# Long branch A of a two-branch encoder layer: three of eight units transposed by VectorE and DRAM, with TensorE's order held

## The chip, the cores and the metric

The kernel runs on one core of one Trainium2 chip. The metric is the device time of one execution in microseconds (us), median of the runs. TensorE (PE) multiplies matrices, VectorE (DVE) and ScalarE (ACT) work elementwise, GpSimd (POOL) helps them, SyncE (SP) issues most DMAs. Lines such as L829 are lines of the kernel before.

## The reference

One encoder layer runs on two sequences with the same weights: `x_prompt` (1024 tokens) and `x_sample` (512 tokens), width 1024, all in float32.

```python
z = rmsnorm(x) @ W_in   # q_A k_A v_A q_B k_B v_B gate_A gate_B
o_A = grouped-query attention: 8 query heads in 2 groups of 4, one key/value head a group,
      head width 64, softmax over all keys, no mask
o_B = neighbourhood attention on the 64-wide token grid, with a position bias
mix = (sigmoid(gate_A) * (o_A @ W_pA) + sigmoid(gate_B) * (o_B @ W_pB)) @ W_out
x = x + mix;  x = x + relu(rmsnorm(x) @ W_up)**2 @ W_down;  y = rmsnorm(x)
```

What the change touches is `o_A` of the 1024-token sequence: for each group, softmax(q k^T / 8) v with 4 heads x 1024 queries x 1024 keys.

## The kernel before

Every float32 operand is used as a sum of two fp32r parts, a rounded one ("hi") and the rest ("lo"), and a product is made of two or three matmuls (`mm3`: hi*hi, hi*lo, lo*hi; the helper `mul`, L212, issues each). The function `run` does the attention part of one sequence, the 512-token one first (`NB` = 1), then the 1024-token one (`NB` = 2, `N` = "s1"). After both comes the MLP for all tokens.

For each of the two groups `g`, a phase "R" projects and rotates q, k and v, and a phase "A" does the attention (L773 to L804 and on). In phase A of the long sequence:

- A **unit** is one head with 512 queries: 4 heads x 2 query blocks = 8 units a group. `NT` = 8 key chunks of 128.
- `s_tile(u, j)` makes the scores of 128 queries against 1024 keys: four 512-column matmuls into a two-bank PSUM tile `s` (two such tiles exist), a VectorE maximum (L788), a ScalarE Exp with row sums (L791), a VectorE reciprocal (L793) and a GpSimd multiplication in place (L794). The result `p` has queries on partitions; eight buffers of it exist.
- For PV the keys must be on partitions. For each key chunk `kc`, TensorE transposes four 128x128 blocks into one PSUM bank (L829), ScalarE copies it as the rounded part (L834), and VectorE subtracts for the rest (L835).
- `pv(u, kc, hi, lo)` adds two 512-column matmuls into the unit's accumulator bank (L805, L806), two chunks behind the transposes (`LAG`). After the eighth, `finish_o` adds the two halves on ScalarE and VectorE (L474, L483) and writes 128 KB to DRAM.
- `fill.pull(n)` takes n steps of other TensorE work: here the gate projection (`gate`), three 512-column matmuls a step.
- In unit u, the four score tiles of unit u+1 are made in chunks 0, 1, 3 and 4.

PSUM has eight banks: four for the two score tiles and four (`mm`) for transposes, accumulators and the gate's sums. A pool of eleven 8 KiB-per-partition buffers (`slot`) holds two activation tiles, q, k and v (four), the gate's weights and whatever comes next.

The order of instructions on each engine is set by a scheduler that works at build time: among instructions that are ready by its own reckoning it takes the one that comes first in the program. `tc.keep_in_program_order` chains an instruction to the earlier ones so marked on the same engine; `tc.issue_after(x)` puts an instruction behind x on x's engine. While `held_pe` is not empty, `mul` chains all TensorE work. Before the change only branch B of the long sequence sets it (the neighbourhood attention, phase "B"), and there most units are already transposed in another way: VectorE transposes 32x32 blocks in place (L1100), the tile is written to DRAM (`tbs`, L1103), read back with its blocks regrouped (`bhs`, L1110), rounded by ScalarE (L1122) and subtracted by VectorE (L1123). For these units the Exp (L1088) writes its result in runs of 32 elements, in an order that makes the regrouping read long runs. The last eight units of branch B are transposed by TensorE, and there the Exp writes every fourth element.

In phase A of the long sequence nothing is held. `put` issues the writes of gates and outputs on ScalarE's DMA queue, unless `slot_no` is set; then they go to a list `later_put`, which SyncE issues later.

## Time and profile before

| | us |
|---|---|
| median of 3 runs | 2127.22 (2126.32 to 2127.64) |
| the profiled execution | 2126.34 |
| its span, first to last instruction | 2124.5 |
| phase A of the long sequence, group 0 | 451.0 to 582.4 in the span |
| phase R of group 1 | 582.4 to 643.5 |
| phase A of the long sequence, group 1 | 643.5 to 774.0 |
| branch B of the long sequence, from its first score matmul | 797.8 on |

The granted TensorE clock is 0.999 of full speed over the span. In the profile's rows, "xcount | busy, mean ns | idle before" gives the time in which at least one instruction of a group ran, the mean duration of one, and how long the engine sat idle just before them with what ended that. Durations of matmuls overlap: a matmul starts before the one in front of it has drained, so the time TensorE needs for one is read from start to start. In a timeline row, the first number is the start in the span, the second the duration, and a row with x4 merges four in a run.

### The profile page before, as it was taken

The numbers are of one execution on the slowest core, as the hardware profiler recorded it, in microseconds if no ns is written. First come the engines' busy times: TensorE is split into PE (matmuls) and PEld (weight loads), VectorE is DVE, ScalarE is ACT, GpSimd is POOL, SyncE is SP. The second block draws the span as 40 slices with busy tenths as digits, with TensorE's granted clock in tenths as the row PEclk, the third lists the DMA queues.
The fourth block names the chain that finished last, engine by engine and source line by source line (L and its number), as shares of the span: only waits on it lengthen the run. The fifth ranks groups of instructions, "written<-read, shape, count | busy, mean of one in ns | idle before, by whom it ended". The sixth has DMA issues, their size and how long they took to land.

```text
span 2124.5 us, 31728 instructions
## 1 busy us (share of the span) xinstructions
PE 2096.5 (99%) x10871; PEld 1839.0 (87%) x10871; DVE 1480.0 (70%) x2793; ACT 1145.7 (54%) x2487; POOL 363.3 (17%) x446
## 2 busy tenths in 40 slices
PE   9999999999999999999999999999999999999998
PEld 8888778888898888887888999999999988888887
DVE  6666786777647756777873877778777777669563
ACT  6665653666666745556531566666565643334452
POOL 2232310332232314443101100002000000000000
PEclk9999999999999999999999999999999999999999
DMA  6436557530122136876563656568454899688561
GB/s 191 133 99 200 160 150 256 192 86 23 49 70 87 45 84 193 241 224 193 172 227 124 199 181 206 163 230 214 156 162 146 272 350 341 213 280 278 164 204 64
DMA packets 336104, 372.92 MB, mean 176 GB/s; under 512 B 31039, under 2 KB 267207, under 8 KB 335943
## 3 DMA queue, kind: packets, MB, share of 16 engines
q1 hardware_dynamic: 297463, 305.60, 45.6%
q10 hardware_dynamic: 31328, 45.11, 6.2%
q0 software_dynamic: 7152, 20.19, 3.5%
q8 instruction: 86, 1.41, 0.3%
q14 instruction: 75, 0.61, 0.1%
HBM read 274.29 MB, written 97.32 MB: 175 GB/s over the span
## 4 chain that ended last, share of the span: by engine, by line
PE 52%; DVE 1%; issue 0%; ACT 0%; POOLq 0%; POOL 0%; ACTq 0%; DVEq 0%
PE dn L212 20%; PE ua L212 6%; PE ud L212 6%; PE uc L212 6%; PE ops L212 4%; PE ub L212 3%; PE ppbs L212 2%; PE ppas L212 2%; PE dnf L212 2%; PE pt L353 1%; PE obs L212 0%; PE ptbs L1132 0%; ACT pbs L1088 0%; PE sbs L212 0%; DVE A L1458 0%
## 5 line engine op out<-in xcount | busy, mean ns | idle before, releaser
L212 PE MATMUL dn<-wd,ah 128*128 128x512 f32 x1248 | 384.2, 389 | 0.0
L212 PEld LDWEIGHTS dn<-wd,ah 128*128 128x128 f32 x1248 | 234.2, 188 | 48.7
L212 PE MATMUL dn<-wd,al 128*128 128x512 f32 x624 | 242.8, 389 | 0.0
L1457 ACT ACTIVATE ah<-ar 128x512 fp32r<-128x512 f32 x168 | 104.4, 627 | 206.7 <-PE dn L212 185.6
L212 PE MATMUL gpss<-xs_0h,w_gs 128*128 128x512 f32 x512 | 189.4, 402 | 0.8 <-DVE ot_Bs L471 0.4
L1458 DVE TENSOR_TENSOR al<-ar,ah 128x512 fp32r<-128x512 f32 x168 | 114.1, 687 | 76.4 <-ACT ah L1457 66.6
L212 PE MATMUL ud<-B,A 128*128 128x384 f32 x768 | 143.7, 334 | 0.7 <-DVE c L1575 0.7
L212 PE MATMUL uc<-B,A 128*128 128x384 f32 x768 | 143.7, 334 | 0.0
L212 PE MATMUL ua<-B,A 128*128 128x384 f32 x768 | 138.8, 334 | 0.0
L212 PEld LDWEIGHTS dn<-wd,al 128*128 128x128 f32 x624 | 117.1, 188 | 24.2
L794 POOL TENSOR_SCALAR ps<-ps,rls 128x1024 f32<-128x1024 f32 (+1 forms) x96 | 96.8, 1009 | 228.4 <-DVE rls L793 213.8
L212 PEld LDWEIGHTS ud<-B,A 128*128 128x128 f32 x768 | 134.0, 188 | 1.1 <-DVE c L1575 1.1
L212 PEld LDWEIGHTS uc<-B,A 128*128 128x128 f32 x768 | 134.1, 188 | 0.2 <-ACT A L1457 0.2
L834 ACT ACTIVATE pths<-pTs 128x512 fp32r<-128x512 f32 x160 | 94.1, 597 | 73.9 <-PE pTs L829 71.3
L212 PEld LDWEIGHTS ua<-B,A 128*128 128x128 f32 x768 | 133.7, 188 | 0.2
L835 DVE TENSOR_TENSOR ptls<-pTs,pths 128x512 fp32r<-128x512 f32 x160 | 107.5, 686 | 37.7 <-ACT pths L834 36.7
L212 PE MATMUL ops<-wh_os,mgs 128*128 128x512 f32 x384 | 119.4, 390 | 0.0
L788 DVE TENSOR_REDUCE nms<-ss 128x1 f32<-128x1024 f32 (+1 forms) x96 | 99.8, 1040 | 25.0 <-PE ss L786 24.5
L212 PEld LDWEIGHTS gpss<-xs_0h,w_gs 128*128 128x128 f32 x512 | 96.1, 188 | 19.0 <-DVE w_gs L206 0.7
L791 ACT ACTIVATE ps<-ss,nms 128x1024 f32<-128x1024 f32 (+1 forms) x96 | 93.3, 972 | 32.1 <-DVE nms L788 26.2
L180 POOL TENSOR_TENSOR rs_f<-ms_f,mhalf 128x1 f32<-128x1 f32 x6 | 4.0, 667 | 590.7 <-DVE ms_f L176 590.7
L829 PEld LDWEIGHTS pTs<-ident,ps 128*128 128x128 f32 x640 | 78.0, 140 | 28.4 <-POOL ps L794 4.4
(287 smaller groups left out, 5144.2 us busy)
## 6 DMA issues: line engine op xcount, KB each, us to landing
ar<-ud SPq DMA_DIRECT2D x120, 512.0 KB, 5.4
br<-in_w_mlp_down_dram SPq DMA_DIRECT2D x72, 512.0 KB, 5.3
rawu<-in_w_mlp_up_dram SPq DMA_DIRECT2D x64, 512.0 KB, 4.1
ud<-c ACTq DMA_DIRECT2D x128, 192.0 KB, 3.6
raw_gs<-in_w_in_dram SPq DMA_DIRECT2D x32, 512.0 KB, 3.9
ud<-cs SPq DMA_DIRECT2D x64, 192.0 KB
tbs<-pbs SPq DMA_DIRECT2D x24, 384.0 KB, 4.8
bhs<-tbs SPq DMA_DIRECT2D x24, 384.0 KB, 3.7
```

What stands on the lines that cost most here:

```text
L180: nc.gpsimd.tensor_tensor(r[:, :n], m[:, :n], mhalf[:, :n], op=ALU.pow)
L212: op = nc.tensor.matmul(out, a, b, **kw)
L353: nc.tensor.transpose(halves[c // 4][:, (c % 4) * P : (c % 4 + 1) * P], t[:, c * P : (c + 1) * P], ident)
L788: nc.vector.tensor_reduce(nm_, s, axis=AX.X, op=ALU.max, negate=True)
L791: op = nc.scalar.activation(p, s, AF.Exp, bias=nm_, accum_out=l)
L794: nc.gpsimd.tensor_scalar(p, p, rl, 1.0, op0=ALU.mult, op1=ALU.mult)
L829: nc.tensor.transpose(pt[:, j * P : (j + 1) * P], PP[u, j][:, kc * P : (kc + 1) * P], ident)
L834: nc.scalar.activation(hi, pt, AF.Copy)
L835: nc.vector.tensor_tensor(lo, pt, hi.bitcast(F32), op=ALU.subtract)
L1457: nc.scalar.activation(hi, src, AF.Copy)
L1458: nc.vector.tensor_tensor(lo, src, hi.bitcast(F32), op=ALU.subtract)
```

## The change

Units 1, 3 and 5 of each group of the long sequence are "turned". For them:

- the Exp reads every fourth column of the PSUM tile in its inner order and writes runs of 32 (`of`, `to`);
- `turn` transposes the tile's 32x32 blocks in place on VectorE (128 x 1024) and writes it to DRAM (512 KB); it is placed inside the next score tile, between the maximum and the Exp (`between`);
- `fetch` reads it back regrouped, two slots later, into a buffer for two tiles; both DMAs are on SyncE's queue, chained;
- `rounded` makes the rounded part on ScalarE, behind the latest Exp, and the rest by a subtract in place: tiles 0 and 2 on GpSimd, 1 and 3 on VectorE;
- `pv_pair` multiplies two tiles (256 queries) at a time: 8 chunks x 2 parts, 16 matmuls of 256 columns, with a stride in the moving operand.

Only the five other units are transposed by TensorE. `step` is one such unit, with its transposes in eight slots, one a key chunk. In the steps of units 0, 2 and 4 the slots carry the score tiles of the turned unit (0 to 3) and of the next plain one (4 to 7), and two gate pulls in the first four slots and one in the others. The first pair of a turned unit is multiplied at the end of the step, the second in slot 1 of the next one. In the step of unit 6 the tiles of unit 7 come in slots 0, 1, 3 and 4.

In both groups TensorE's order is held from the first score tile to the end, and gates and outputs are written by SyncE from `later_put`. The short sequence keeps the old loop. The diff, without the lines that only rename:

```diff
@@ -184,7 +184,7 @@
...
     def note(engine, op):
-        if held_pe:
+        if "B" in held_pe:
             firm[engine].append(op.ins)
@@ -772,9 +772,10 @@
...
                 units = [(h, qb) for h in range(4) for qb in range(NB)]
-                PP = {}
-
-                def s_tile(u, j):
+                PP, tA, fA, hA, last_exp = {}, {}, {}, {}, [None]
+                turned = {units[i] for i in (1, 3, 5)} if NB == 2 else set()
+
+                def s_tile(u, j, between=None):
                     h, qb = u
@@ -782,13 +783,20 @@
...
                         ks = slice(kb * 512, kb * 512 + 512)
-                        nc.tensor.matmul(s[:, ks], lhs, kT[:, 0, ks], start=True, stop=False)
-                        nc.tensor.matmul(s[:, ks], lhs, kT[:, 1, ks], start=False, stop=True)
+                        mul(s[:, ks], lhs, kT[:, 0, ks], start=True, stop=False)
+                        mul(s[:, ks], lhs, kT[:, 1, ks], start=False, stop=True)
                     nm_ = sml.tile([P, 1], F32, tag="nm", name=f"nm{nm}")
                     nc.vector.tensor_reduce(nm_, s, axis=AX.X, op=ALU.max, negate=True)
+                    if between is not None:
+                        between()
                     p = ph.tile([P, T], F32, tag="P", name=f"p{nm}", bufs=8)
                     l = sml.tile([P, 1], F32, tag="l", name=f"l{nm}")
-                    op = nc.scalar.activation(p, s, AF.Exp, bias=nm_, accum_out=l)
+                    to, of = p, s
+                    if u in turned:
+                        to = p.rearrange("p (b k i) -> p k b i", b=4, i=32)
+                        of = s.rearrange("p (k i b) -> p k b i", b=4, i=32)
+                    op = nc.scalar.activation(to, of, AF.Exp, bias=nm_, accum_out=l)
+                    last_exp[0] = op.ins
                     rl = sml.tile([P, 1], F32, tag="rl", name=f"rl{nm}")
@@ -802,18 +810,121 @@
...
                     o = o_of[u]
-                    nc.tensor.matmul(o, vhl[:, kc, :], hi, start=(kc == 0), stop=False)
-                    nc.tensor.matmul(o, vhl[:, kc, :], lo, start=False, stop=(kc == NT - 1))
+                    mul(o, vhl[:, kc, :], hi, start=(kc == 0), stop=False)
+                    mul(o, vhl[:, kc, :], lo, start=False, stop=(kc == NT - 1))
                     if kc == NT - 1:
-                        r0 = (g * 4 + h) * HD
-                        finish_o(o, 512, oad[r0 : r0 + HD, qb * 512 : qb * 512 + 512], ph, f"A{N}_{g}_{h}_{qb}")
-
+                        end_o(u)
+
+                def end_o(u):
+                    h, qb = u
+                    r0 = (g * 4 + h) * HD
+                    cs = slice(qb * 512, qb * 512 + 512)
+                    finish_o(o_of.pop(u), 512, oad[r0 : r0 + HD, cs], ph, f"A{N}_{g}_{h}_{qb}")
+
+                def turn(u, j):
+                    p = PP[u, j]
+                    blocks = p.rearrange("p (n i) -> p n i", i=32)
+                    tc.keep_in_program_order(nc.vector.transpose(blocks, blocks))
+                    tA[u, j] = dram.tile([P, 4, T // 4], F32, name=f"ta{N}_{g}_{u[0]}_{u[1]}_{j}")
+                    tc.keep_in_program_order(nc.sync.dma_start(tA[u, j], p.rearrange("p (b w) -> p b w", b=4)))
+
+                def fetch(u, j):
+                    of = tA.pop((u, j)).rearrange("(a i) b w -> (i b) a w", i=32)
+                    if j % 2 == 0:
+                        fA[u, j // 2] = slot([P, 2, T], F32R, f"fa{N}_{g}_{u[0]}_{u[1]}_{j // 2}")
+                    to = fA[u, j // 2][:, j % 2].bitcast(F32).rearrange("p (a w) -> p a w", a=4)
+                    tc.keep_in_program_order(nc.sync.dma_start(to, of))
+
+                def rounded(u, j, eng):
+                    if j % 2 == 0:
+                        hA[u, j // 2] = slot([P, 2, T], F32R, f"ha{N}_{g}_{u[0]}_{u[1]}_{j // 2}")
+                    p, hi = fA[u, j // 2][:, j % 2], hA[u, j // 2][:, j % 2]
+                    with tc.issue_after(last_exp[0]):
+                        nc.scalar.activation(hi, p.bitcast(F32), AF.Copy)
+                    tc.keep_in_program_order(
+                        eng.tensor_tensor(p, p.bitcast(F32), hi.bitcast(F32), op=ALU.subtract)
+                    )
+
+                def pv_pair(u, pr):
+                    if pr == 0:
+                        o_of[u] = mm(f"o{N}_{g}_{u[0]}_{u[1]}")
+                    o = o_of[u][:, pr * 256 : pr * 256 + 256].rearrange("p (n i) -> p n i", i=32)
+                    hi, lo = hA.pop((u, pr)), fA.pop((u, pr))
+                    for kc in range(NT):
+                        for i, t in enumerate((hi, lo)):
+                            mv = t.rearrange("p j w -> p (j w)").rearrange("p (n k i) -> p k n i", n=8, i=32)[:, kc]
+                            mul(
+                                o,
+                                vhl[:, kc, :],
+                                mv,
+                                start=(kc + i == 0),
+                                stop=(kc + i == NT),
+                                skip_group_check=True,
+                            )
+                    if pr == 1:
+                        end_o(u)
+
+                if NB == 2:
+                    held_pe.append("A")
+                    slot_no[0] = 0
                 for j in range(4):
...
                 LAG = 2
-                for ui, u in enumerate(units):
+
+                def put_later():
+                    slot_no[0] += 1
+                    while later_put and later_put[0][0] < slot_no[0] - 1:
+                        tc.keep_in_program_order(nc.sync.dma_start(*later_put.pop(0)[1:]))
+
+                def step(u, late, mine, nxt, pulls):
+                    h, qb = u
+                    hooks, extra = {}, {}
+                    if mine is not None:
+                        hooks = {j + 1: partial(turn, mine, j) for j in range(4)}
+                        extra = {3 + j: [partial(fetch, mine, j)] for j in range(4)}
+                        extra[5].append(partial(rounded, mine, 0, nc.gpsimd))
+                        extra[6].append(partial(rounded, mine, 1, nc.vector))
+                        extra[7] = [partial(rounded, mine, 2, nc.gpsimd)]
+                        s_list = [(mine, j) for j in range(4)] + [(nxt, j) for j in range(4)]
+                    else:
+                        s_list = [(nxt, 0), (nxt, 1), None, (nxt, 2), (nxt, 3)] if nxt is not None else []
+                    for kc in range(NT):
+                        pt = mm(f"pT{N}_{g}_{h}_{qb}_{kc}")
+                        for j in range(4):
+                            op = nc.tensor.transpose(
+                                pt[:, j * P : (j + 1) * P], PP[u, j][:, kc * P : (kc + 1) * P], ident
+                            )
+                            tc.keep_in_program_order(op)
+                        hi = ph.tile([P, 512], F32R, tag="pth", name=f"pth{N}_{g}_{h}_{qb}_{kc}", bufs=3)
+                        lo = ph.tile([P, 512], F32R, tag="ptl", name=f"ptl{N}_{g}_{h}_{qb}_{kc}", bufs=3)
+                        nc.scalar.activation(hi, pt, AF.Copy)
+                        nc.vector.tensor_tensor(lo, pt, hi.bitcast(F32), op=ALU.subtract)
+                        queue.append((u, kc, hi, lo))
+                        if kc < len(s_list) and s_list[kc] is not None:
+                            s_tile(*s_list[kc], hooks.get(kc))
+                        for f in extra.get(kc, ()):
+                            f()
+                        if kc == 0 and late is not None:
+                            rounded(late, 3, nc.vector)
+                        fill.pull(pulls[kc])
+                        if kc == 1 and late is not None:
+                            pv_pair(late, 1)
+                        if len(queue) > LAG:
+                            pv(*queue.pop(0))
+                        if kc % 4 == 3:
+                            put_later()
+                    if mine is not None:
+                        pv_pair(mine, 0)
+
+                if NB == 2:
+                    for i in (0, 2, 4):
+                        late = units[i - 1] if i else None
+                        step(units[i], late, units[i + 1], units[i + 2], (2, 2, 2, 2, 1, 1, 1, 1))
+                    step(units[6], units[5], None, units[7], (1, 1, 1, 1, 1, 1, 1, 0))
+                    step(units[7], None, None, None, (1, 1, 1, 1, 1, 0, 1, 0))
+                for ui, u in enumerate(units if NB == 1 else ()):
                     h, qb = u
@@ -845,6 +956,12 @@
...
                     pv(*item)
+                if NB == 2:
+                    held_pe.clear()
+                    slot_no[0] = None
+                    for _, dst, src in later_put:
+                        nc.sync.dma_start(dst, src)
+                    later_put.clear()
@@ -1187,7 +1304,7 @@
...
                 slot_no[0] = 0
-                held_pe.append(1)
+                held_pe.append("B")
                 fill.pull(3)
```

## The prediction

> **What bounds the kernel now.** I read the page first, then the busy times by stretch, the groups inside one group's stretch, and the timeline there.
>
> ```profile
> span 2124.5 us, 31728 instructions
> ...
> PE 2096.5 (99%) x10871; PEld 1839.0 (87%) x10871; DVE 1480.0 (70%) x2793; ACT 1145.7 (54%) x2487; POOL 363.3 (17%) x446
> ```
> ```profile
> 451.00:582.40 131.40, 130.57 (x696) 106.23 (x695) 95.33 (x152) 85.74 (x152) 36.98 (x32) 1.00 0.16 48
> ```
> TensorE (PE) is occupied for the whole span, and so it is in the stretch of long branch A's first group (131.4 us; columns PE, PEld, DVE, ACT, POOL busy, clock, DMA share, GB/s); the second group's is like it. VectorE has 36 us of slack there, ScalarE 46, the DMA engines 84%. An edit pays only by what it takes off TensorE's own list, minus the new times at which TensorE stands. The groups of the first stretch:
>
> ```profile
> L835 DVE TENSOR_TENSOR ptls<-pTs,pths 128x512 fp32r<-128x512 f32 x64 | 42.9, 687 | 15.6 <-ACT pths L834 15.2
> L788 DVE TENSOR_REDUCE nms<-ss 128x1 f32<-128x1024 f32 x32 | 38.9, 1217 | 8.8 <-PE ss L786 8.8
> L829 PE MATMUL pTs<-ident,ps 128*128 128x128 f32 x256 | 38.9, 273 | 0.4 <-DVE ptls L835 0.3
> L834 ACT ACTIVATE pths<-pTs 128x512 fp32r<-128x512 f32 x64 | 37.6, 597 | 30.2 <-PE pTs L829 29.2
> L794 POOL TENSOR_SCALAR ps<-ps,rls 128x1024 f32<-128x1024 f32 x32 | 37.0, 1156 | 85.0 <-DVE rls L793 84.4 <-PE pTs L829 0.6
> L791 ACT ACTIVATE ps<-ss,nms 128x1024 f32<-128x1024 f32 x32 | 35.7, 1115 | 10.0 <-DVE nms L788 8.4 <-DVE rls L793 1.4
> ```
> TensorE waits for nothing worth naming (0.4 us before its transposes), although its order is that of a scheduler, which is free to put other matmuls wherever one would wait. Matmul durations overlap, so I price TensorE by start-to-start:
>
> ```profile
> 519.32 0.60 PE L829 MATMUL pTs<-ident,ps 128*128 128x128 f32 x4
> 519.68 0.48 PE L212 MATMUL gpss<-xs_0h,w_gs 128*128 128x512 f32 x1
> 519.99 0.39 PE L212 MATMUL gpss<-xs_0l,w_gs 128*128 128x512 f32 x1
> 520.22 0.39 PE L212 MATMUL gpss<-xs_0h,w_gs 128*128 128x512 f32 x1
> ```
> Four transposes hold the array 0.36 us, and the matmul behind them 0.31 instead of 0.23: 0.44 us for a set of four. A 512-column matmul is 0.23.
>
> **The change, part by part.**
>
> *Transposes removed.* Three units in each of two groups drop eight sets each: 48 x 0.44 = -21.1 us.
>
> *Turned PV.* Its matmuls have 256 columns; the nearest rows are those of the other branch:
>
> ```profile
> 878.47 0.39 PE L212 MATMUL gpss<-xs_0h,w_gs 128*128 128x512 f32 x1
> 878.70 0.89 PE L212 MATMUL obs<-bhs,vss 128*128 128x256 f32 x6
> 879.42 0.87 PE L212 MATMUL sbs<-kBs,qBs 128*128 128x384 f32 x4
> ```
> Six take 0.72 us, 0.12 each, also in runs of 32 elements. A unit now has 32 of them (3.84 us) for 16 of 0.23 (3.68): 6 x 0.16 = +1.0 us.
>
> *Order held: the start of a group.* What TensorE must now wait for is the chain from a score tile to its normalised rows (reduce, Exp, reciprocal, GpSimd's scaling). Two of these chains, a short one and, by its ends, a usual one:
>
> ```profile
> 461.40 0.39 PE L786 MATMUL ss<-kTs,qTs 128*128 128x512 f32 x1
> ...
> 461.82 1.23 DVE L788 TENSOR_REDUCE nms<-ss 128x1 f32<-128x1024 f32 x1 [0.97 <-PE ss L786]
> ...
> 463.08 1.12 ACT L791 ACTIVATE ps<-ss,nms 128x1024 f32<-128x1024 f32 x1 [1.06 <-DVE nms L788]
> ...
> 464.57 1.12 POOL L794 TENSOR_SCALAR ps<-ps,rls 128x1024 f32<-128x1024 f32 x1 [0.24 <-DVE rls L793]
> ```
> ```profile
> 517.94 0.39 PE L786 MATMUL ss<-kTs,qTs 128*128 128x512 f32 x1
> ...
> 522.08 1.13 POOL L794 TENSOR_SCALAR ps<-ps,rls 128x1024 f32<-128x1024 f32 x1 [0.30 <-DVE rls L793]
> ```
> From the last score matmul's start: 4.3 us (461.40 to 465.69) and 5.3 (517.94 to 523.21). At a group's start the held order has after it only itself, two pulls of gate work (6 x 0.23) and three transposes that do not need the tile (0.33): 1.94 us. TensorE stands 4.3 - 1.94 = 2.4 us, twice: +4.7. Before, the next unit's scores filled this.
>
> *Order held: unit boundaries.* A plain step carries eight score tiles now, four for the turned unit and four for the next plain one. The last is made in slot 7; before, it was there by slot 4. TensorE has after it 0.23 + one pull 0.69 + PV 0.46 + sixteen turned matmuls 1.94 + three transposes 0.33 = 3.65 us, against a chain of 5.3: it stands 1.65 us; at best 0.65 (4.3). There are three such boundaries a group: 6 x 1.65 = +9.9 us.
>
> *The detour of the turned rows.* VectorE turn, write, read back, ScalarE rounding, a subtract. Rows of the nearest operations:
>
> ```profile
> L1643 DVE TENSOR_TENSOR ar<-ar,ar 128x1024 f32<-128x1024 f32 x36 | 44.0, 1223 | 31.3 <-DMA ar<-ud 31.3
> ...
> L1100 DVE STREAM_TRANSPOSE pbs<-pbs 128x768 f32<-128x768 f32 x24 | 23.2, 966 | 0.0
> ...
> L365 POOL TENSOR_TENSOR B<-ta,B 128x512 fp32r<-128x512 f32 x12 | 15.5, 1294 | 120.6 <-ACT B L362 120.2
> ...
> L365 DVE TENSOR_TENSOR B<-ta,B 128x512 fp32r<-128x512 f32 x12 | 9.8, 855 | 1.6 <-ACT B L362 1.6
> ```
> ```profile
> tbs<-pbs SPq DMA_DIRECT2D x24, 384.0 KB, 4.8
> bhs<-tbs SPq DMA_DIRECT2D x23, 384.0 KB, 3.7
> ```
> ```profile
> L1088 ACT ACTIVATE pbs<-sbss,nmbs 128x384 f32<-128x384 f32 x40 | 24.4, 610 | 17.3 <-DMA tbs<-pbs 12.6 <-DVE nmbs L1059 2.8 <-issue 1.7
> L1122 ACT ACTIVATE bhs<-bhs 128x768 fp32r<-128x768 f32 x18 | 15.2, 845 | 23.5 <-DMA bhs<-tbs 23.4
> ```
> Scaled by size: turn 1.29 us, subtract 1.22 on VectorE and 2.6 on GpSimd, write 6.4, read 4.9; rounding 1.13. A slot is 0.44 + 0.92 scores + 1.38 (or 0.69) pulls + 0.46 PV = 3.2 us (2.5 from slot 4); slot 1 has 1.94 more from the earlier turned unit, so slot 3 begins at 11.5. Score tile 3 of the turned unit has its last matmul there at 12.4, is normalised at 17.7, turned at 19.0. SyncE's queue holds the read of tile 1 behind the write of tile 3, issued at 19.0, so that read lands at 23.9; with rounding and subtract tile 1 is ready at 26.3. TensorE asks for it at 24.5 and then needs 1.94 + 0.33 to where the boundary's wait stands: 28.6, beside 28.4 for the tile chain (last matmul at 23.1, and 5.3). So the two waits overlap, and the detour adds 0.2.
>
> *The Exp of the turned tiles* now reads PSUM in steps of four elements. No row shows such a read. The one step-of-four access is a write to SBUF in the other branch (its last eight units):
>
> ```profile
> L1088 ACT ACTIVATE pbs<-sbss,nmbs 128x384 f32<-128x384 f32 x14 | 13.7, 996 | 7.4 <-DVE nmbs L1059 7.3
> ```
> 996 ns against 610 in the units that write runs of 32 (above): 1.0 ns an element more. On 1024 elements that is 1.1 to 2.2 us; I see no reason for a gain. At 2.2 the detour is 1.1 later, so 0.2 to 1.3 a boundary; between the ends I take 0.6: 6 x 0.6 = +3.6 us. [...]
>
> *What is hidden.* VectorE in such a step: 8 x (0.69 + 1.22 + 0.16) + 4 x 1.29 + 2 x 1.22 + two finishes of 0.68 = 25.5 us of about 28.5. GpSimd: 8 x 1.16 + 2 x 2.6 = 14.5. ScalarE: 8 x (0.60 + 1.12) + 4 x 1.13 + small = 20, with four Exps at 2.2 some 24. All fit; VectorE's margin of 3 us is the thinnest, and without it the subtracts would be the next late thing. A 512-column subtract with both inputs in SBUF, beside GpSimd's, took 855 ns against 687 from PSUM: 0.17, so two a step cost the margin some 0.4 to 0.7. Gate and output writes go from ScalarE's queue to SyncE's, half a unit to a unit later, long after their data is there; nobody reads them in this branch. Of eleven 8 KiB buffers six are held and two are the gate's; the fourth one a turned unit needs comes free after its first pair, and 1.13 + 2.6 us of rounding fit before its second pair, 5.7 us into the next step. The next stage's weights lose their early buffers and load in the last two steps (some 29 us), else they would cost about 6.
>
> Sum: -21.1 + 1.0 + 4.7 + 9.9 + 3.6 = -1.9 us, of the profiled execution's 2126.3 (span 2124.5): 2124.4. The median of the runs, 2127.2, is 0.9 above it, so 2125.3.
>
> **The rivals.** *The waits stay at their floor.* If every boundary finds the short chain and the detour hides, the return is 1.0 + 4.7 + 6 x 0.65: -21.1 + 9.6 = -11.5, so 2115.7. For it: the other branch already works like this, and its turned units leave no such gaps in TensorE's rows. Against it: there the tiles have a whole unit's slack, here the last slot.
>
> *ScalarE becomes the late one (slower).* Exps at 2.2 us in slots 0 to 3, and in-order roundings that stand before a read has landed (23.4 us in 18 roundings, 1.3 each, in the row above; and 12.6 us of Exps waiting for a write to free its rows). Then both pairs of a turned unit come 1.1 late in the open: 12 x 1.1 = 13.2 instead of 3.6 gives -1.9 + 9.6 = +7.7, so 2134.9. It decides as soon as the turned Exps read 2 us and ScalarE's wait for the reads passes some 2 us a step; half of it gives 2130.
>
> *The change does not do what it says:* roundings could not be placed in the held order and TensorE idles in whole steps; nothing here points to it.
>
> **How the numbers follow.** A measurement here can tell 0.2%, 4.3 us: faster is below 2122.9, slower above 2131.5. Forecast (most of the gain given back; 2119 to 2132, since a boundary may cost 1 us more or less) 0.42; floor 0.26; ScalarE late 0.29; the last 0.03. Of the forecast's 0.42, 0.10 is faster and 0.03 slower; of ScalarE's 0.29, 0.23 is slower, the rest is its milder half. Faster: 0.26 + 0.10 = 0.36; slower: 0.03 + 0.23 + 0.03 = 0.29; no change that can be told: 0.35. Cases of both signs hold the chance, so the range reaches from just below the floor's 2115.7 to just above 2134.9: 2114 to 2136.
>
> **What would show it.** Right: per group 160 transposes instead of 256 on TensorE; gaps of 2.4 us before a group's first transposes and 1.5 to 2.5 before those of the third, fifth and seventh unit, released by GpSimd's scaling or by the subtracts; group stretches near 130 us. Turned Exps at 1.1 or 2.2 us settle the read. Wrong: gaps under 1 us (floor), or gaps in the middle of steps, released by ScalarE or by the reads (slower).

## The result and the profile after

| | median us | runs | ratio to before, 95% interval |
|---|---|---|---|
| before | 2127.14 (2126.33 to 2127.64) | 4 | |
| after | 2161.96 (2160.74 to 2165.41) | 4 | 1.0167 (1.0149 to 1.0184) |

The changed kernel is 35 us slower, above the upper end of the forecast's range (2136). The page of after, its head:

```profile
span 2160.8 us, 31552 instructions
...
PE 2098.2 (97%) x10775; PEld 1838.3 (85%) x10775; DVE 1495.1 (69%) x2781; ACT 1143.8 (53%) x2463; POOL 397.3 (18%) x458
```

The span grew by 36.3 us. Busy times by stretch, after: long branch A's first group, and two stretches inside it, each the slots ahead of a step's end and a part of the wait there (columns PE, PEld, DVE, ACT, POOL, then granted clock, DMA share, GB/s):

```profile
451.00:600.70 149.70, 131.57 (x650) 105.83 (x650) 103.41 (x147) 86.73 (x147) 52.84 (x38) 0.95 0.38 124
480.00:491.90 11.90, 10.40 (x51) 7.79 (x49) 10.40 (x16) 8.96 (x15) 6.06 (x5) 1.00 0.84 273
510.00:526.00 16.00, 13.68 (x69) 10.83 (x67) 14.88 (x19) 11.36 (x19) 6.82 (x5) 1.00 0.67 226
```

The group takes 149.7 us instead of 131.4, the second 148.6 instead of 130.5: the two are the whole difference. TensorE has 46 instructions fewer and often stands, that is, it issues nothing because it waits. Its clock, 1.00 in this stretch before, is 0.95. And just ahead of a step's end VectorE is busy 87 to 93%, against 69% over the group (103.41 of 149.70).

The groups of the new operations (after, first group; the last two rows are from the DMA view, with KB and the median us from issue to landing):

```profile
L798 ACT ACTIVATE ps<-ss,nms 128x1024 f32<-128x1024 f32 x32 | 35.7, 1114 | 21.8 <-DVE nms L789 17.4 <-DMA vds<-vts 2.5 <-issue 1.8
...
L827 DVE STREAM_TRANSPOSE ps<-ps 128x1024 f32<-128x1024 f32 x12 | 14.9, 1239 | 2.8 <-POOL ps L802 2.6
...
L845 POOL TENSOR_TENSOR fas<-fas,has 128x1024 fp32r<-128x1024 f32 x6 | 14.2, 2372 | 3.9 <-ACT has L843 3.8
...
L843 ACT ACTIVATE has<-fas 128x1024 fp32r<-128x1024 f32 x12 | 12.7, 1055 | 5.4 <-PE os L212 4.9 <-DMA fas<-tas 0.5
...
L845 DVE TENSOR_TENSOR fas<-fas,has 128x1024 fp32r<-128x1024 f32 x6 | 7.9, 1323 | 1.6 <-ACT has L843 0.8 <-DMA fas<-tas 0.8
```
```profile
tas<-ps SPq DMA_DIRECT2D x12, 512.0 KB, 2.9
fas<-tas SPq DMA_DIRECT2D x12, 512.0 KB, 5.0
```

No part is much dearer than forecast (turn 1.24 us, GpSimd's subtract 2.37, rounding 1.06, read 5.0; VectorE's subtract at a mean of 1.32 is 0.1 above its forecast), and the Exps that read PSUM in steps of four are in the first row, 1.11 us like the others (1.106 to 1.120 over all 32). What went wrong is when these parts stand in the queues. The timeline of after at the end of the first step:

```profile
488.18 1.19 PE L212 MATMUL ss<-kTs,qTs 128*128 128x512 f32 x4
...
488.65 6.70 SPq L879 DMA_DIRECT2D zgs<-sgs  x3
...
489.69 1.11 ACT L798 ACTIVATE ps<-ss,nms 128x1024 f32<-128x1024 f32 x1
489.87 2.36 POOL L845 TENSOR_TENSOR fas<-fas,has 128x1024 fp32r<-128x1024 f32 x1
...
490.13 0.39 PE L212 MATMUL os<-ptls,vhls 128*128 128x512 f32 x1
...
490.77 1.05 ACT L843 ACTIVATE has<-fas 128x1024 fp32r<-128x1024 f32 x1
...
491.72 1.11 ACT L798 ACTIVATE ps<-ss,nms 128x1024 f32<-128x1024 f32 x1
491.86 1.45 DVE L845 TENSOR_TENSOR fas<-fas,has 128x1024 fp32r<-128x1024 f32 x1 [0.78 <-ACT has L843]
...
491.88 0.39 PE L212 MATMUL os<-has,vhls 128*128 128x256 f32 x1 [1.37 <-ACT has L843]
492.21 3.18 POOL L802 TENSOR_SCALAR ps<-ps,rls 128x1024 f32<-128x1024 f32 x2
...
493.41 0.36 PE L212 MATMUL os<-fas,vhls 128*128 128x256 f32 x1 [1.14 <-DVE rls L801]
...
494.41 0.60 ACT L460 ACTIVATE sgs<-gpss 128x512 f32<-128x512 f32 x1 [1.49 <-DMA zgs<-sgs]
...
495.79 1.05 PE L896 MATMUL pTs<-ident,ps 128*128 128x128 f32 x4
```

Read it from TensorE. It has issued its last plain PV at 490.13 and wants the first turned pair (the sixteen matmuls of `pv_pair`) from about 490.4. What it waits for is tile 1. SyncE issued the read of that tile at 485.51, the first of three in this row of the view of SyncE alone:

```profile
485.51 3.09 SPq L836 DMA_DIRECT2D fas<-tas  x3
```

At 5.0 us a read it lands at about 490.5, so the way out and back alone is already as late as TensorE's demand. ScalarE is then in the Exp of slot 6 and begins the rounding at 490.77, 0.3 later. VectorE's subtract starts at 491.86 and takes 1.45 us, beside a subtract of GpSimd that ends at 492.23. TensorE stands 1.5 us for the rounded part and 1.4 for the rest (491.88, 493.41).

Two more things come due just behind. One is the next unit's last tile, whose scaling ends at 495.39, 6.4 us from its last score matmul at 488.98, where the forecast had 5.3. Its Exp (491.72) stood behind the rounding, and GpSimd, late by its own subtract, then needed 3.18 us from 492.21 for two scalings that take 1.13 each when alone. The longest scaling is seen here (duration in ns, min/median/max):

```profile
L802 POOL TENSOR_SCALAR ps<-ps,rls x32: 1108/1126/2095, 459.4 to 586.2; 128x1024 f32<-128x1024 f32 x32
```

In each of the six steps with a turned unit, one scaling that runs beside VectorE's subtract takes 2.0 to 2.1 us. The other thing is a sigmoid at 494.41, which holds a PSUM bank and waited for a gate write that SyncE issued late. Had the pair been ready at once, it would have ended at about 492.3, and the transposes behind it would have stood some 2.8 us for the tile instead (an estimate from these rows, if the tile came no sooner). That is a likely reason why, below, many a single remedy wins nothing.

TensorE's list, summed from start to start over both groups (0.227 us for a 512-column matmul, 0.120 for 256, 0.109 for a transpose; what an interval has above that is a stand if it is a single long one, half clock if it is one of a run at about twice its time):

| us | before | after | forecast of the difference |
|---|---|---|---|
| work at full clock | 259.4 | 240.3 | -20.1 |
| stands | 1.2 | 45.0 | +18.2 |
| half clock | 0.8 | 12.4 | 0 |

The differences, -19.1 + 43.8 + 11.6, make the 36.3 us of the span. Where a short wait is counted as a stand is a choice that moves the split by some 2 us. Of the stands 5.0 are at the two starts of a group, 20.0 at the six first pairs (ahead of the first matmul and of the second), 7.6 at the second pairs, and some 12 in the slots (score banks, VectorE's subtracts of transposed rows).

The half clock is seen at a group's start (after):

```profile
465.02 0.33 PE L896 MATMUL pTs<-ident,ps 128*128 128x128 f32 x1 [1.01 <-POOL ps L802]
466.39 0.33 PE L896 MATMUL pTs<-ident,ps 128*128 128x128 f32 x1 [1.04 <-POOL ps L802]
466.47 1.34 PE L212 MATMUL ss<-kTs,qTs 128*128 128x512 f32 x4
467.60 0.63 PE L212 MATMUL gpss<-xs_1h,w_gs 128*128 128x512 f32 x1
468.03 0.63 PE L212 MATMUL gpss<-xs_1l,w_gs 128*128 128x512 f32 x1
```

Two stands of 1.2 us within 2.8 us, and from 467.60 the matmuls start 0.43 us apart instead of 0.23, until 470.8. The granted clock is 0.50 from 467.33 to 470.75; there are nine such stretches, each of 3.41 us, in the two groups.

### The profile page after: what moved, and what is told of

It reads as the page before. It is cut to its first block, busy times and chain, and to the rows that moved or that the text cites. A ratio compares the mean times of both kernels' runs of the same rounds, so it can differ in the third digit from the quotient of the medians.

```text
span 2160.8 us, 31552 instructions
## 1 busy us (share of the span) xinstructions
PE 2098.2 (97%) x10775; PEld 1838.3 (85%) x10775; DVE 1495.1 (69%) x2781; ACT 1143.8 (53%) x2463; POOL 397.3 (18%) x458
## 5 line engine op out<-in xcount | busy, mean ns | idle before, releaser
L802 POOL TENSOR_SCALAR ps<-ps,rls 128x1024 f32<-128x1024 f32 (+1 forms) x96 | 102.6, 1071 | 222.0 <-DVE rls L801 198.6
L212 PE MATMUL ss<-kTs,qTs 128*128 128x512 f32 x320 | 99.2, 424 | 4.9 <-ACT ps L798 2.9
L212 PE MATMUL gpss<-xs_0l,w_gs 128*128 128x512 f32 x256 | 100.7, 393 | 0.0
L212 PE MATMUL gpss<-xs_1h,w_gs 128*128 128x512 f32 x256 | 92.7, 402 | 0.9 <-ACT sgs L460 0.9
```

The source lines that it names most:

```text
L212: op = nc.tensor.matmul(out, a, b, **kw)
L802: nc.gpsimd.tensor_scalar(p, p, rl, 1.0, op0=ALU.mult, op1=ALU.mult)
```

## The experiments

Each is the changed kernel with the edit shown; line numbers behind an edit shift. "Held" and "free" say whether TensorE's order is held. "Stands" and "half clock" are the sums of the table above, over both groups, in us. They come from one profiled execution each, which in e6, e7 and e10 was slower than the median (2165.25, 2169.61 and 2116.99). How much half clock there is differs between executions of one program: e7's four took 2157.80 to 2169.61, the faster the higher their mean granted clock (0.997 to 0.990).

| run | order | median us | ratio to before (95%) | stands | half clock |
|---|---|---|---|---|---|
| e1 hold alone | held | 2133.54 | 1.0029 (1.0018 to 1.0040) | 7.3 | 2.6 |
| e2 no turn | held | 2157.56 | 1.0141 (1.0126 to 1.0156) | 43.2 | 9.4 |
| e3 fetch ahead | held | 2162.14 | 1.0167 (1.0150 to 1.0184) | 46.3 | 9.9 |
| e4 busy wait | held | 2156.65 | 1.0139 (1.0124 to 1.0154) | | |
| e5 order free | free | 2125.41 | 0.9992 (0.9982 to 1.0001) | 18.1 | 1.9 |
| e6 pulls late | held | 2161.58 | 1.0164 (1.0149 to 1.0179) | 44.7 | 15.7 |
| e7 fetch ahead, VectorE | held | 2163.21 | 1.0161 (1.0144 to 1.0177) | 48.9 | 13.9 |
| e8 slot order | held | 2143.49 | 1.0075 (1.0060 to 1.0090) | 31.0 | 6.6 |
| e9 slot order and two steps | held | 2138.76 | 1.0061 (1.0045 to 1.0076) | 28.1 | 1.8 |
| e10 the same | free | 2113.68 | 0.9940 (0.9928 to 0.9953) | 9.2 | 0.3 |
| e11 no rounding | held | 2132.78 | 1.0027 (1.0017 to 1.0037) | 24.7 | 4.9 |
| e12 slot order | free | 2124.55 | 0.9986 (0.9977 to 0.9995) | 16.4 | 3.0 |
| e13 and late subtract | free | 2116.48 | 0.9952 (0.9939 to 0.9964) | 9.6 | 0.6 |
| e14 and early writes | free | 2115.71 | 0.9949 (0.9935 to 0.9962) | 8.3 | 0.7 |
| e15 early writes alone | held | 2162.51 | 1.0171 (1.0157 to 1.0185) | 45.4 | 10.9 |

**e1: the hold without turned units.**

```diff
-                turned = {units[i] for i in (1, 3, 5)} if NB == 2 else set()
+                turned = set()
...
+                    for i in range(8):
+                        nxt = units[i + 1] if i < 7 else None
+                        step(units[i], None, None, nxt, (1, 1, 1, 0, 1, 1, 1, 0))
```

> TensorE's order is held as in the changed kernel, but no unit is turned: eight plain steps a group, with the score tiles and pulls where the kernel before has them. Theory (the turned units' deadlines at the end of a step cost the time, and TensorE's clock, which halves for some 3 us after a stand of about 2.4 us, adds to it): only the stand at a group's start is left, 2 x (2.4 + 1.5 for the clock), so about 2135. Rival 1 (VectorE's queue is the late one in the turned steps): the same, 2135. Rival 2 (a held order by itself costs the time, whatever is turned): 2150 or more.

Measured 2133.54, 6.3 us over before: the two starts of a group stand 2.4 and 2.5 us, each with a half-clock stretch behind it, and hardly anything else does. So a held order with no unit turned costs that and no more, and the rival that put the whole loss on the hold is out. The other two theories expected the same number here, and this run does not part them.

**e2: VectorE's turn left out.**

```diff
-                    tc.keep_in_program_order(nc.vector.transpose(blocks, blocks))
```

> The changed kernel without VectorE's 24 turning instructions (12 a group, 1.24 us each); the rows are written, read back and used as they are, so the output lacks the turn within blocks. Rival 1 (VectorE, 93% busy in the slots ahead of the worst stand, is late): the stands at the end of the steps go to under 1 us each and with them the half clock, so 2135 to 2140. Theory (the rows' way out and back and the order of the roundings behind the Exps set the stand): the rows are only one turn earlier, 6 x 1.2 and a part of the clock's loss, so about 2150.

Measured 2157.56: 4.4 us of 35. Neither number came. 30 us less on VectorE take 1.8 us off the stands, so VectorE's total is not the limit; but the theory's 1.2 us a step did not come through either. The half clock is 3.0 us less, in one execution.

**e3: the read of tile 1 ahead of the write of tile 3, and its rounding a slot earlier.**

```diff
-                        extra[6].append(partial(rounded, mine, 1, nc.vector))
+                        extra[4] = []
+                        extra[5].append(partial(rounded, mine, 1, nc.vector))
...
+                        if kc == 4 and mine is not None:
+                            fetch(mine, 1)
```

> The changed kernel with the read of the turned tile 1 issued on SyncE ahead of the write of tile 3 (at the start of slot 4), and its rounding on ScalarE put behind the Exp of slot 5, not that of slot 6. Theory (the way out and back and the order of the roundings): the stand ahead of the first turned matmuls falls from 2.9 to 4.2 us to some 1.3 to 2, and the half clock behind it goes, so 2162 - 10 - 8 = about 2144. Rival 1 (VectorE's queue): the subtract and the reduces are as late as before, 2158 to 2164.

Measured 2162.14: nothing won. The timeline says why:

```profile
487.28 2.36 POOL L845 TENSOR_TENSOR fas<-fas,has 128x1024 fp32r<-128x1024 f32 x1
...
488.17 2.55 DVE L845 TENSOR_TENSOR fas<-fas,has 128x1024 fp32r<-128x1024 f32 x1
488.19 0.39 PE L212 MATMUL os<-has,vhls 128*128 128x256 f32 x1 [0.24 <-ACT has L843]
...
490.82 0.36 PE L212 MATMUL os<-fas,vhls 128*128 128x256 f32 x1 [2.24 <-DVE rls L801]
```

The rounded parts are in time, as wanted; but VectorE's subtract now runs beside GpSimd's and takes 2.55 us instead of 1.2. It ends 1.08 us behind GpSimd's (490.72 and 489.64), as if it had done nothing until then. The pair stands 2.5 us for it after 0.4 for its first matmul, and 2.9 in the next steps.

**e7: the same, with the subtract of tile 0 on VectorE too.**

```diff
-                        extra[5].append(partial(rounded, mine, 0, nc.gpsimd))
+                        extra[5].append(partial(rounded, mine, 0, nc.vector))
```

> The kernel with the read of tile 1 ahead of the write of tile 3 (which stood as long as the changed kernel), and besides the subtract of tile 0 on VectorE instead of GpSimd, so that none of GpSimd's 2.4 us subtracts runs beside VectorE's of the first pair. There VectorE's subtract took 2.4 to 2.55 us beside GpSimd's, 1.2 alone. Theory (that doubling ate what the earlier read won): the two subtracts take 2.4 us in sequence, the first turned matmuls start some 1.2 us sooner in each of six steps, and some of the half clock goes: about 2150 to 2154. Rival (VectorE's queue is full): 1.2 us more on it a step leaves the stands as they are, 2160 to 2166.

Measured 2163.21. The stands of the pairs did fall, to 2.6, 1.7 and 1.7 us in the first group, but the transposes behind them now stand 1.1, 3.0 and 1.6, so in the whole nothing is won. The forecast from the theory missed, since it looked at one of the things that are late.

**e6: the pulls later in the step.**

```diff
-                        step(units[i], late, units[i + 1], units[i + 2], (2, 2, 2, 2, 1, 1, 1, 1))
+                        step(units[i], late, units[i + 1], units[i + 2], (1, 1, 2, 2, 1, 1, 2, 2))
```

> The changed kernel with the twelve pulls of gate work of a step spread (1,1,2,2,1,1,2,2) over its slots instead of (2,2,2,2,1,1,1,1): 1.4 us more between the making of the turned tiles and the end of the step. Theory (a chain of fixed length against a deadline): each end-of-step stand falls by some 1.4 us, with it the half clock behind the shorter ones: 6 x 1.4 + 4 = 12, so about 2150. Rival (VectorE's rate): slots of 2.5 us ask 3.3 us of VectorE, its queue grows as the slots shrink, and nothing is won: 2160 or more.

Measured 2161.58. The rival's outcome: giving the detour 1.4 us more slack did nothing, so it is not a chain of fixed length against a deadline. That it stretches with the queues it passes is the rival's reading, which this run fits and does not show by itself.

**e4: matmuls in the stands.**

```diff
+                def busy(to, n):
+                    for _ in range(n):
+                        mul(to, vhl[:, 0, :], kT[:, 0, 0:512], start=True, stop=True)
...
                     if pr == 0:
                         o_of[u] = mm(f"o{N}_{g}_{u[0]}_{u[1]}")
+                        busy(o_of[u], 12)
...
+                        if kc == 0 and u == units[0]:
+                            busy(pt, 10)
```

> The changed kernel with matmuls put where TensorE stands longest, whose product is overwritten: 12 of 512 columns (2.7 us) ahead of the first pair of each turned unit, 10 (2.3 us) ahead of a group's first transposes. Theory (a stand also halves the clock for some 3 us, about 1.3 us lost each, 8 such stands): the stands are filled and the clock stays, so 2162 - 10 = about 2151, with the clock at 1.00 in both groups; VectorE gets its next score tile no sooner. If the clock is not tied to the stands: 2162 or a little more where the matmuls outlast the stand (2162 to 2168), with the clock at 0.95.

Measured 2156.65. The clock of the first group (stretch from 3 us ahead of its first score matmul to its end, as in the rows of e10 and e11 below):

```profile
450.79:598.07 147.28, 137.68 (x695) 111.13 (x696) 103.89 (x147) 86.62 (x147) 52.98 (x38) 0.98 0.39 126
```

0.98 instead of 0.95, two half-clock stretches left instead of nine, and 5.3 us won by adding work: the half clock does come of the stands. It is a part of the loss, about a third (11.6 of 36.3 us); what fills the stands here is no useful work.

**e5: the order free.**

```diff
-                    held_pe.append("A")
...
-                            tc.keep_in_program_order(op)
```

> The changed kernel with TensorE's order left to the scheduler as before (neither its matmuls nor its transposes are held); the turned units and all their steps stay. Theory (the stands come of deadlines that the held order sets a slot or two too early): the scheduler moves other matmuls into the places where TensorE stood, 2127 - 9 for the transposes saved less some stands, 2118 to 2130. Rival (the turned rows are late by their own chain in any order, VectorE's queue among it): the stands stay, 2150 to 2165.

Measured 2125.41, 36.6 us less than the same work held, and not to be told from before. So the turned rows are early enough for some order, and not for the one written. It is not TensorE's order alone that differs: the scheduler places the other engines too, and in the first group the sequences of operations on VectorE, ScalarE and GpSimd are not those of the changed kernel. The 36.6 us are the price of the written order as a whole. What the scheduler leaves is 18 us of stands, which is about what the removed transposes bring.

**e11: no rounding of the turned rows.**

```diff
-                    with tc.issue_after(last_exp[0]):
-                        nc.scalar.activation(hi, p.bitcast(F32), AF.Copy)
-                    tc.keep_in_program_order(
-                        eng.tensor_tensor(p, p.bitcast(F32), hi.bitcast(F32), op=ALU.subtract)
-                    )
+                    hA[u, j // 2] = fA[u, j // 2]
```

> The changed kernel without the rounding of the turned rows: no ScalarE copies, no subtracts on GpSimd and VectorE (48 operations of 1.05 to 2.4 us left out over both groups); the read-back rows serve as both parts, so the output of the turned units is wrong. TensorE's work, the writes and reads are as in the changed kernel. Theory (the end-of-step stand is the chain of the next unit's last score tile, 5.3 us when alone, 7.2 us when roundings and subtracts stand in the queues, and the turned rows' own): the boundary stands fall to the 1.65 us forecast from the chain alone, and none lasts long enough to halve the clock: 2162 - 14 - 7 - 9 = about 2132. Rival (the reads land late; the roundings only wait for them): the stands stay near 3 us, 2150 or more.

The products of the turned units are no longer those of the reference, since both parts are the same rows. Measured 2132.78, the theory's 2132: with 48 operations gone from ScalarE, VectorE and GpSimd, 29 of the 35 us are gone, while TensorE's order, the turns, the writes and the reads are all there. First the row of its first group, then the end of its first step:

```profile
451.24:588.09 136.85, 127.19 (x650) 102.81 (x651) 93.98 (x141) 75.45 (x135) 37.52 (x32) 0.98 0.42 136
```
```profile
491.15 2.17 PE L212 MATMUL os<-fas,vhls 128*128 128x256 f32 x16 [0.42 <-DMA fas<-tas]
...
494.45 0.60 ACT L460 ACTIVATE sgs<-gpss 128x512 f32<-128x512 f32 x1 [2.30 <-DMA zgs<-sgs]
...
495.20 0.63 PE L889 MATMUL pTs<-ident,ps 128*128 128x128 f32 x4 [1.88 <-ACT sgs L460]
```

The pair stands 0.6 us for a read, the reads being just in time; and then the next in line shows: the transposes stand 1.9 us for a PSUM bank that a sigmoid holds, which waited 2.3 us for a late gate write. So the theory's number came, but not by its account: the six boundaries stand between 0.8 and 3.3 us, not 1.65 each, and two half-clock stretches follow them. What the run shows is the size of what goes with the roundings, not the way they cost it.

**e8: each slot's order turned round.**

```diff
-                        extra[7] = [partial(rounded, mine, 2, nc.gpsimd)]
...
                     for kc in range(NT):
+                        if kc < len(s_list) and s_list[kc] is not None:
+                            s_tile(*s_list[kc], hooks.get(kc))
+                        for f in extra.get(kc, ()):
+                            f()
+                        fill.pull(pulls[kc])
+                        if kc == 0 and late is not None:
+                            pv_pair(late, 0)
+                            rounded(late, 2, nc.gpsimd)
+                            rounded(late, 3, nc.vector)
+                        if kc == 2 and late is not None:
+                            pv_pair(late, 1)
                         pt = mm(f"pT{N}_{g}_{h}_{qb}_{kc}")
...
-                    if mine is not None:
-                        pv_pair(mine, 0)
```

> The changed kernel with each slot's order turned round: score tile and pulls first, then the four transposes; the first turned pair after the pulls of the next step's slot 0, the roundings of tiles 2 and 3 behind it, the second pair in slot 2. Everything that TensorE must wait for is asked for 2.3 us later, at no cost in instructions. Theory (deadlines): the stand at a group's start goes, the end-of-step stands fall from 2.9 to 4.2 us to 0.6 to 1.9, and no stand is long enough to halve the clock: 2162 - 5 - 14 - 12 = about 2131. Rival (VectorE's rate): the stands return in the slots, 2145 or more.

Measured 2143.49: 18 us of the 31 that were forecast, and just under the rival's 2145. The first pair still stood:

```profile
485.11 6.81 SPq L879 DMA_DIRECT2D zgs<-sgs  x3
...
490.97 0.60 ACT L460 ACTIVATE sgs<-gpss 128x512 f32<-128x512 f32 x1 [0.71 <-DMA zgs<-sgs]
...
491.62 0.39 PE L212 MATMUL os<-has,vhls 128*128 128x256 f32 x1 [2.36 <-ACT sgs L460]
```

Its rows are ready by then, and it is the bank behind the late gate write that it waits for.

**e9 and e10: the slot order, writes at once on ScalarE's queue, the subtract of tile 3 and the second pair a slot later; held, then free.** Against e8; e10 besides drops the hold, as e5 does.

```diff
-                    slot_no[0] = 0
...
                             rounded(late, 2, nc.gpsimd)
-                            rounded(late, 3, nc.vector)
-                        if kc == 2 and late is not None:
+                        if kc == 1 and late is not None:
+                            rounded(late, 3, nc.vector)
+                        if kc == 3 and late is not None:
                             pv_pair(late, 1)
...
-                        if kc % 4 == 3:
-                            put_later()
```

> The kernel with each slot's order turned round, and besides: gate and output writes issued on ScalarE's queue at once, as in the kernel before, instead of late on SyncE's; the subtract of tile 3 on VectorE one slot later, after GpSimd's of tile 2, and the second pair in slot 3. In the kernel with the slot order alone the first pair stood 2.5 us for a gate PSUM bank whose sigmoid waited for a late gate write, and the transposes of slot 1 stood 1.9 to 3.3 us behind VectorE's subtract, which took 1.9 to 2.0 us beside GpSimd's. Theory (these two are what is left): 2143.5 - 2 x 1.5 - 6 x 1.5 - some clock = about 2128. Rival (VectorE's rate): the stands move on, within 4 us of 2143.

> The same program order as the kernel with the slot order turned round, the writes on ScalarE's queue and the subtract of tile 3 a slot later, with TensorE's order left to the scheduler. Theory: the scheduler fills what is left of the stands; the free order of the changed kernel gave 2125.4 with 18 us of stands, of which about 8 stood behind a VectorE operation slowed beside GpSimd or a tile behind it: 2114 to 2120. Rival (the scheduler already has the freedom, the program's order matters little): 2123 to 2127.

Held it takes 2138.76, 4.7 us less than e8 where 15 were forecast, so the rival (within 4 us) was nearer; free 2113.68, faster than both kernels: 13.5 us below before. The first group of e10:

```profile
451.12:576.49 125.37, 122.91 (x649) 100.31 (x650) 102.64 (x147) 86.70 (x147) 52.40 (x38) 1.00 0.47 150
```

The turned units and the computing operations on every engine are those of the changed kernel, and the clock is at 1.00.

**e12 to e15: which of the two steps.** e12 is e8 with TensorE's order free; e13 adds only the step of the subtract and the second pair, e14 only the writes'; e15 is the changed kernel, held, with only the writes at once. In the order of the runs:

```diff
e12, to e8
-                    held_pe.append("A")
...
-                            tc.keep_in_program_order(op)
...
e13, to e12
-                            rounded(late, 3, nc.vector)
-                        if kc == 2 and late is not None:
+                        if kc == 1 and late is not None:
+                            rounded(late, 3, nc.vector)
+                        if kc == 3 and late is not None:
...
e14 to e12, e15 to the changed kernel
-                    slot_no[0] = 0
...
-                        if kc % 4 == 3:
-                            put_later()
```

> The kernel with the slot order turned round (writes still late on SyncE's queue, the subtract of tile 3 in slot 0, the second pair in slot 2), with TensorE's order left to the scheduler. It parts the 11.7 us between the free changed kernel (2125.4) and the free one with all three steps (2113.7). If the slot order gives them (deadlines moved away in the program's order): 2114 to 2117. If the writes' queue and the subtract placed a slot later, out of GpSimd's way, give them (the contention): 2120 to 2126.

> The free kernel with the slot order turned round, and the subtract of tile 3 a slot later and the second pair in slot 3; the writes stay late on SyncE's queue. Contention theory (VectorE's subtract beside GpSimd's holds up the subtracts of TensorE's transposed rows: 6 stands of 1.4 to 2.1 us): 2115 to 2118. Writes theory: 2122 to 2125.

> The free kernel with the slot order turned round, and the gate and output writes on ScalarE's queue at once; the subtract of tile 3 stays in slot 0 beside GpSimd's. Contention theory: 2121 to 2125. Writes theory (a late write holds a sigmoid's buffer and a PSUM bank): 2115 to 2118.

> The changed kernel, order held, with only the gate and output writes on ScalarE's queue at once. Contention theory (its stands are of the roundings' and subtracts' places in the queues): 2157 to 2163. Writes theory: 2150 or less.

Free, the slot order alone gives 2124.55, hardly less than the changed kernel's 2125.41 free; either step brings it to 2116; both together give 2113.68, which the intervals do not part from either alone. So each theory's number came for its own step, and they do not add up: neither can be named as the one cause. Nor does e13 show the contention alone, since it moves the second pair as well, and tile 3 of the first turned unit of each group still has a subtract of 2.5 us. In the changed kernel itself the writes cost nothing (e15, 2162.51); that something else is as late there fits, but wasn't shown. What the subtract's step takes away is seen in e12:

```profile
494.87 2.40 POOL L845 TENSOR_TENSOR fas<-fas,has 128x1024 fp32r<-128x1024 f32 x1
...
495.01 3.33 DVE L845 TENSOR_TENSOR fas<-fas,has 128x1024 fp32r<-128x1024 f32 x1
498.26 0.68 DVE L911 TENSOR_TENSOR ptls<-pTs,pths 128x512 fp32r<-128x512 f32 x1
499.00 0.66 PE L905 MATMUL pTs<-ident,ps 128*128 128x128 f32 x4 [1.86 <-DVE ptls L911]
```

VectorE's subtract takes 3.33 us, ending 1.07 behind GpSimd's; the subtract of the transposed rows waits behind it, and TensorE's transposes wait for that.

## Why the prediction was wrong

- *Transposes removed, turned PV* (-21.1 and +1.0): right. Work at full clock fell by 19.1 us for a forecast of 20.1.
- *Start of a group* (2.4 us, twice): right, 2.44 and 2.51 us, in two pieces, as the tile before the last is late too. The half clock behind each was not in it.
- *Unit boundaries and detour* (9.9 + 3.6 = 13.5): too small, 20.0 us at the first pairs. The step that failed is "So the two waits overlap, and the detour adds 0.2": two chains were added up from durations as if each had its engines to itself. By the forecast's own times the pair waits 1.8 us (26.3 less 24.5); in the first group it waited 2.9, 4.2 and 2.9. That the read leaves no time for rounding and subtract was right (in the first step it landed about when TensorE asked). What was missing stands in the queues behind it: an Exp ahead of the rounding (0.3 us in the first step, some 0.9 in the second at 5.0 us a read), a subtract stretched beside GpSimd's (1.45) or begun 0.8 us after its rounding had ended (second step, 526.26 and 527.05). The tile's chain took 6.4 us in the first step, not 5.3, since the rounding, GpSimd's subtract and a scaling stretched beside VectorE's subtract stood in it. That two waits are at about the same place, so that one hides the other, was right; e7 shows it, where the stand moves from the pair to the transposes.
- *What is hidden* (0): this is the term that was mis-sized most. "All fit" was drawn from sums over a step; the 20 us of stands inside the slots and at the second pairs come of the order within it. VectorE was busy 93% over 16 us up to a step's end. The paragraph named VectorE's margin as the thinnest, and then let it cost nothing. The price of a subtract beside GpSimd's was taken as 0.17 us from a mean; one that meets it whole costs up to 2.1 (3.33 against 1.2). The next stage's weights are indeed hidden: phase R of group 1 takes 60.9 us after, 61.1 before.
- *The clock*: no term at all. It is 11.6 us, a third of the loss; the forecast's own stands of 2.4 us would have brought some of it (e1: 1.8 us more than before).
- *Exps in steps of four* (+3.6 within the sum): no cost, the Exps took 1.11 us. No run shows the 2.2 us of the forecast's upper end, which was an estimate from a stepped write. So 3.6 of the 13.5 had a wrong reason, and without them the boundaries are mis-sized by 10 us rather than 6.5.
- *Gate and output writes* "long after their data is there": in the changed kernel they indeed cost nothing (e15), but the buffer that a write frees was overlooked; in the free kernel the early writes are worth 8.8 us (e12 against e14).
- *The rivals.* The slower one had the right place, in-order roundings, and the wrong reason (Exps at 2.2 us), and priced it at 2134.9. The floor, 2115.7, is near what e13, e14 and e10 reach, but with the order free, which is not its case. Turned rows ready in time for another order, and not for this, was a case that was not listed.

What stays open: e11 shows that 29 of the 35 us go with the 48 rounding operations in the held order, and e5 that a free order makes all of the loss good. How the 29 divide among ScalarE's copies and GpSimd's and VectorE's subtracts, and between their places in the queues and the stretching of one beside the other, wasn't tried; since a stand moves when one remedy is applied (e7), they need not divide.

## What to carry to other kernels

Where the bound engine's order is fixed by hand, walk every helper engine's queue up to each deadline in order, operation by operation; a sum of busy time that fits the step says nothing about the end of it. Where several things come due within a few microseconds, a remedy for one may win nothing, so look for the change that moves them all (the slot order, the free order) before concluding that a cause is refuted. And allow for a half clock behind stands of TensorE: here one of 2.31 us (e5) was followed by it, 2.30 (e5) and 3.10 us (e9) were not, and each stretch in the changed kernel cost 1.4 us (12.4 over nine).

## What the runs showed of the hardware

- TensorE's granted clock fell to half behind some stands and not behind others of about the same length. In the changed kernel a stand of 2.44 us in two pieces was followed by 3.41 us at a granted clock of 0.50 (467.33 to 470.75), and each of its nine half-clock stretches in the two groups lasts 3.41 us. Of single stands (from start to start) in e5, one of 2.31 us (ahead of 520.57) was followed by half clock (the turned matmuls at 521.21 and 521.40 last 0.40 and 0.42 us), and one of 2.30 (ahead of 713.85) was not (0.28 each). Neither was one of 2.02 us in e12 (ahead of 499.00), nor one of 3.10 in e9 (granted clock 1.00 from 556 to 563, rows below). So the length of a stand alone does not tell whether the clock falls; what else decides it was not shown.

```profile
556.47 0.39 PE L212 MATMUL gpss<-xs_0h,w_gs 128*128 128x512 f32 x1
559.79 0.66 PE L901 MATMUL pTs<-ident,ps 128*128 128x128 f32 x4 [2.94 <-DVE ptls L908]
```

- A VectorE subtract with both inputs in SBUF took 1.2 us alone (1.216 at 503.12 in the changed kernel, with GpSimd idle), and beside a GpSimd subtract 1.45 us in the changed kernel (491.86), 2.55 in e3 and 3.33 in e12, ending 1.08, 1.08 and 1.07 us behind GpSimd's end. It goes the other way too: in the changed kernel GpSimd's scaling took 2.0 to 2.1 us beside a VectorE subtract, 1.13 alone.
- An Exp on ScalarE that reads PSUM in steps of four elements and writes runs of 32 took 1.11 us on 1024 columns, as one in order (1.106 to 1.120 over all 32 of the first group). The forecast had bounded it by 2.2, an estimate from the other branch's Exp that writes SBUF in steps of four (996 ns on 384 columns, against 610 in runs of 32).
